# A hybrid GLA / S5 trunk on one core: z with both parts of u in one 512-column matmul, heads written in S5 order, background rates moved

## The chip, the cores and the metric

The program runs on one core of a Trainium2 chip. The metric is the device time of one execution in microseconds (us); lower is better. Runs of the kernel before: 1853.9, 1856.19 and 1862.4 us, median 1856.19.

## What is computed

Two layers on 256 tokens of width 2048, each a mixer with adaLN modulation around it and a LayerNorm after it. Layer 0 is gated linear attention (GLA), layer 1 an S5 state-space mixer. The part that the change touches is the first mixer:

```
u = x * (1 + scale) + shift                      # adaLN, from ada_w and c
q, k, v, z, g = split(u @ w_in)                  # 1024, 1024, 4096, 4096, 16 columns
o = chunked gated linear attention(q, k, v, g)   # 4 heads, 1024 values each
o = o * rsqrt(mean(o^2 over a head) + eps) * norm_g
h = (o * silu(z)) @ w_out
x = layer_norm(alpha * x + (1 + gate) * h)
```

The S5 layer projects the new x to its own u and z, runs the recurrence, multiplies gelu(y) by sigmoid(y @ w_glu + b), then by silu(z), and projects out.

## The kernel before

Everything large is a product with a weight matrix in float32 that must keep float32's accuracy. So each operand is cut in two parts of a shorter format: hi is the value cast, lo is the rest. `split` (L142) does that for each weight block of 2 x 128 rows by 512 columns: ScalarE casts hi (L145), VectorE subtracts to lo (L146). `hilo` (L327) does the same for activations. A product is then hi x hi + hi x lo + lo x hi, three matmuls.

Three helpers issue them. `mv_step` (L159) keeps the activations stationary and streams 512 weight columns. `st_step` (L171) keeps a 128 x 128 weight block stationary and streams 256 tokens: per feature block f (4) and k (2) it issues three matmuls of 256 columns (L180 to L182), all into the first half of a bank. `st_wide` (L184) streams hi and lo of the activations side by side in one matmul of 512 columns (L192), so that a bank's two halves hold two partial sums; a second matmul of 256 columns (L193) adds weight lo x activation hi to the first half. Whoever reads the bank must add the halves. `st_wide` needs activations in `Pairs` (hi and lo of each k next to each other), `st_step` takes `Parts` (hi tiles and lo tiles).

The stages, in order: u0 is made and v, q, k are projected in four blocks of k (`vqk_steps`, the last block runs 36 steps); the gate and the decayed state products follow (`gla_gate`, qs, sts); then the z stage, 8 groups of 512 columns with 8 steps each (L837 to L853); then `out_proj(0, ...)` with 4 column groups of 16 steps; then the S5 layer, whose GLU stage (L1241 on) uses `st_wide`. Inside the z stage the heads' work is taken from the queue `hq`: `o_step` makes 128 output features of a head and their squares, `rms` and `inv` the root and its reciprocal, `scale` multiplies, and `head_fin` multiplies by silu(z).

The S5 layer wants tokens in another order, (s c) with s = 8 steps of a chunk first. Before, z was written in that order by the Silu (L849), the heads' outputs stayed in token order, and `head_fin` (L833) read them with steps. PSUM has a pool `mm` of 5 banks; a z group holds 4 of them. Small tiles come from `s8`, 12 slots of 8 KB.

Besides the main work a list `bg` holds background items: 26 preparation items for S5, then 12 parts of the adaLN weights with 9 items each (`ada_dve`, L275: a load of 512 KB and two multiply-adds of 512 columns on VectorE, L292, or a closing item), 134 in all up to the end of `out_proj(0, ...)`. `pump(rate)` adds the rate to a counter and runs an item whenever it reaches 1. V_RATE holds in the last projection block (36 steps), Z_RATE in z (64), OP_RATE in the output projection (64). `issue_after(last_lo[0])` keeps an item's multiply-adds behind the newest lo on VectorE. What is written first has the better place, but the framework's planner orders each engine's instructions by that place and by its own costs; the engines then run their queues in order. Loads of weights go through SP's queue into a ring of buffers.

Of the kernel before, what the change touches and what calls it, by code (L numbers as in the profile page):

```python
# [8 lines left out]
F32 = mybir.dt.float32  # L9
F32R = mybir.dt.float32r  # L10
AF = mybir.ActivationFunctionType
# [4 lines left out]
P = 128  # L16
# [17 lines left out]
def trunk(ctx, tc, x, c, ln_g, ln_b, ada_w, ada_b, gla_w_in, gla_gate_w2, gla_gate_b, gla_norm_g,  # L34
# [39 lines left out]
    def s8t(name, shape, dt=F32):  # L74
        return s8.tile([P] + shape, dt, tag="s8", name=name)
# [95 lines left out]
    def st_step(banks, u, w, kp, last, first=0):  # L171

        hi, lo = w
        for f in range(4):
            for kk in range(2):
                k = 2 * kp + kk
                wh = hi[:, kk, f * P:(f + 1) * P]
                wl = lo[:, kk, f * P:(f + 1) * P]
                o = banks[f][:, :T]
                PE.matmul(o, lhsT=wh, rhs=u.hi(k), start=(k == first), stop=False)  # L180
                PE.matmul(o, lhsT=wh, rhs=u.lo(k), start=False, stop=False)  # L181
                PE.matmul(o, lhsT=wl, rhs=u.hi(k), start=False, stop=(k == last))  # L182

    def st_wide(banks, u, w, kp, last):  # L184


        hi, lo = w
        for f in range(4):
            for kk in range(2):
                k = 2 * kp + kk  # L190
                fs = slice(f * P, (f + 1) * P)
                PE.matmul(banks[f], lhsT=hi[:, kk, fs], rhs=u.both(k), start=(k == 0), stop=False)  # L192
                PE.matmul(banks[f][:, :T], lhsT=lo[:, kk, fs], rhs=u.hi(k), start=False, stop=(k == last))  # L193
# [128 lines left out]
        for tt in range(2):  # L322
            dma(xr[tt][:, c0:c1], x[0, tt * P:(tt + 1) * P, c0:c1])

    u0 = Parts([s8t(f"u0h{i}", [8, T], F32R) for i in range(2)], [s8t(f"u0l{i}", [8, T], F32R) for i in range(2)])

    def hilo(hi, lo, src):  # L327
        S.copy(hi, src)
# [313 lines left out]
    for part in range(2):  # L642
        for j in range(4):
            bg.extend(ada_dve(1, part, j))
    V_RATE, Z_RATE, OP_RATE = 0.825, 0.944, 0.755
    KEEP = (4, 6)
    GATE_AT = 15
    SCAN_RATE = 1.728
# [140 lines left out]
    y0 = Parts([], [])  # L789


    zt_ = [s8t(f"z{h}", [8, T]) for h in range(4)]
    og, sq = [None] * 4, [None] * 4

    def head(h):
        def o_step(vt_):
            if vt_ == 0:
                og[h] = s8t(f"og{h}", [8, T])
                sq[h] = tp.tile([P, T], F32, tag="sq", name=f"sq{h}", bufs=2)
            f = h * 8 + vt_  # L800
            ps = psx(f"pso{f}")
            PE.matmul(ps[:, 0:256], lhsT=vtok[:, 0, f * P:(f + 1) * P], rhs=sts[:, h, 0:256], start=True, stop=False)
            PE.matmul(ps[:, 128:256], lhsT=vtok[:, 1, f * P:(f + 1) * P], rhs=sts[:, h, 256:384], start=False, stop=True)
            S.activation(og[h][:, vt_, :], ps[:, :T], AF.Identity, scale=gnT[:, f:f + 1])
            if vt_ == 0:
                S.activation(sq[h], ps[:, :T], AF.Square)
            else:
                s_ = tp.tile([P, T], F32, tag="sqt", name=f"sqt{f}", bufs=2)
                S.activation(s_, ps[:, :T], AF.Square)
                V.tensor_tensor(sq[h], sq[h], s_, op=ALU.add)  # L810

        sd = {}

        def rms():
            ps = psx(f"psrms{h}")
            PE.matmul(ps[:, :T], lhsT=ones, rhs=sq[h], start=True, stop=True)
            sd[0] = tp.tile([P, T], F32, tag="sd", name=f"sd{h}", bufs=1)
            S.activation(sd[0], ps[:, :T], AF.Sqrt, scale=1.0 / 1024.0, bias=rmseps)

        def inv():  # L820
            V.reciprocal(sd[0], sd[0])

        def scale(i):
            o = og[h][:, 4 * i:4 * i + 4]
            V.tensor_tensor(o, o, sd[0].unsqueeze(1).to_broadcast([P, 4, T]), op=ALU.mult)

        return [lambda i=i: o_step(i) for i in range(8)] + [rms, inv] + [lambda i=i: scale(i) for i in range(2)]

    def head_fin(h):
        def step(i):  # L830
            sl = slice(4 * i, 4 * i + 4)
            zv = zt_[h][:, sl].rearrange("p f (s c) -> p f s c", s=8)
            V.tensor_tensor(zv, og[h][:, sl].rearrange("p f (c s) -> p f s c", s=8), zv, op=ALU.mult)  # L833
        return [lambda i=i: step(i) for i in range(2)]

    hq = []
    for g in range(8):  # L837
        if g % 2 == 0:
            hq += head(g // 2)
        banks = [psm(f"z{g}{f}") for f in range(4)]  # L840
        for kp in range(8):
            for _ in range(-(-len(hq) // (8 * (2 - g % 2) - kp))):
                hq.pop(0)()
            w = split(wload(win, 2 * kp, 6144 + g * 512, f"z{g}{kp}"), f"z{g}{kp}")
            st_step(banks, u0, w, kp, 15)
            pump(Z_RATE)
        for f in range(4):
            i = (g * 4 + f) % 8
            S.activation(zt_[g // 2][:, i, :].rearrange("p (s c) -> p c s", s=8), banks[f][:, :T].rearrange("p (c s) -> p c s", s=8), AF.Silu)  # L849
        if g % 2 == 1:  # L850
            hq += head_fin(g // 2)
            if g == 1:
                hq += conv(y0, zt_[0], "y0")  # L853
# [516 lines left out]
```

## Time and profile before

| | us |
|---|---|
| median of 3 runs | 1856.19 |
| profiled execution, device time | 1857.15 |
| its span (first to last instruction) | 1855.4 |
| TensorE busy | 1804.1 (97%) |
| VectorE busy | 1425.7 (77%) |
| ScalarE busy | 900.1 (49%) |

The profiled execution is a run of its own, 1.75 us longer than its span. A matmul's duration in the trace is longer than its share of the engine, because matmuls are pipelined: two that follow each other overlap. How fast they go is read from start to start. A row's square brackets hold the idle time of the engine just before the instruction, and what ended it.

### The profile page before, as it was taken

How to read it: one execution, taken by the hardware profiler on the slowest of the kernel's cores; microseconds unless marked ns; L12 is line 12 of the kernel's file. 1: busy time of each engine (PE TensorE's matmuls, PEld its weight loads, DVE VectorE, ACT ScalarE, POOL GpSimd, SP SyncE). 2: the span in 40 equal slices, each digit the busy share in tenths (PEclk: the TensorE clock that was granted, in tenths of full speed). 3: DMA queues.
4: the chain of work that ended last, by engine and by line, in shares of the span. 5: the costliest groups of instructions: out<-in, count | busy, mean ns of one | idle time of the engine just before them, and what ended most of it. 6: DMA issues, size and time to landing. Idle time of an engine off the chain costs nothing.

```text
span 1855.4 us, 33824 instructions
## 1 busy us (share of the span) xinstructions
PE 1804.1 (97%) x13619; PEld 1590.0 (86%) x13619; DVE 1425.7 (77%) x1890; ACT 900.1 (49%) x1252; POOL 65.0 (4%) x76
## 2 busy tenths in 40 slices
PE   6999999999999999999999999999999999999998
PEld 3787798799999888799998899998888888888886
DVE  2788675989989988688899779888677775557556
ACT  3533365655556333654444444555544444444332
POOL 0000000000000000002222110000000000000000
PEclk9999999999999999999999999999999999999998
DMA  9887976689889998565555477899788886668653
GB/s 357 316 270 249 348 252 210 216 296 325 284 287 316 334 352 285 174 199 165 157 164 157 123 207 217 238 241 248 226 271 263 277 272 211 191 187 328 194 188 91
DMA packets 239525, 449.21 MB, mean 242 GB/s; under 512 B 19236, under 2 KB 45278, under 8 KB 238086
## 3 DMA queue, kind: packets, MB, share of 16 engines
q1 hardware_dynamic: 235432, 437.59, 73.5%
q0 software_dynamic: 3168, 8.41, 1.4%
q8 instruction: 107, 1.75, 0.4%
q10 hardware_dynamic: 768, 1.05, 0.2%
q14 instruction: 50, 0.41, 0.1%
HBM read 432.55 MB, written 14.42 MB: 241 GB/s over the span
## 4 chain that ended last, share of the span: by engine, by line
PE 75%; DVE 5%; DMA 3%; ACT 1%; issue 1%; SPq 0%; DVEq 0%; ACTq 0%
PE gl L192 13%; PE gl L193 7%; PE op L168 6%; PE op L169 6%; PE op L167 6%; PE z L182 3%; PE z L180 3%; PE z L181 3%; PE sz L180 3%; PE sz L182 3%; PE sz L181 3%; PE su L180 2%; PE su L181 2%; PE su L182 2%; DMA rb<-rec 1%; PE pswb L1018 1%
## 5 line engine op out<-in xcount | busy, mean ns | idle before, releaser
L146 DVE TENSOR_TENSOR logl<-wgl,higl 128x1024 fp32r<-128x1024 f32 x128 | 156.5, 1224 | 114.7 <-ACT higl L145 113.3
L145 ACT CAST higl<-wgl 128x1024 fp32r<-128x1024 f32 x128 | 134.8, 1054 | 171.2 <-PE gl L192 160.3
L192 PE MATMUL gl<-yp,higl 128*128 128x512 f32 x512 | 179.1, 395 | 0.1
L192 PE MATMUL gl<-yb,higl 128*128 128x512 f32 x512 | 179.1, 395 | 0.0
L145 ACT CAST hio<-wo 128x1024 fp32r<-128x1024 f32 x96 | 101.4, 1057 | 155.1 <-PE op L169 137.2
L146 DVE TENSOR_TENSOR loo<-wo,hio 128x1024 fp32r<-128x1024 f32 x96 | 117.3, 1223 | 65.3 <-ACT hio L145 63.3
L292 DVE SCALAR_TENSOR_TENSOR acc<-wa,cs,acc 128x512 f32<-128x512 f32 x215 | 160.9, 748 | 2.8
L180 PE MATMUL su<-u1h,hisu 128*128 128x256 f32 x512 | 153.0, 300 | 0.0
L180 PE MATMUL sz<-u1h,hisz 128*128 128x256 f32 x512 | 149.6, 292 | 1.2 <-ACT zs L1201 1.2
L180 PE MATMUL z<-u0h,hiz 128*128 128x256 f32 x512 | 148.7, 290 | 0.0
L181 PE MATMUL su<-u1l,hisu 128*128 128x256 f32 x512 | 147.1, 287 | 0.0
L182 PE MATMUL su<-u1h,losu 128*128 128x256 f32 x512 | 146.6, 286 | 0.0
L182 PE MATMUL z<-u0h,loz 128*128 128x256 f32 x512 | 145.0, 283 | 0.9 <-DVE loz L146 0.9
L182 PE MATMUL sz<-u1h,losz 128*128 128x256 f32 x512 | 144.8, 283 | 0.3 <-DVE losz L146 0.3
L181 PE MATMUL sz<-u1l,hisz 128*128 128x256 f32 x512 | 144.8, 283 | 0.0
L181 PE MATMUL z<-u0l,hiz 128*128 128x256 f32 x512 | 144.7, 283 | 0.0
L193 PE MATMUL gl<-yb,logl 128*128 128x256 f32 x512 | 143.1, 280 | 0.0
L193 PE MATMUL gl<-yp,logl 128*128 128x256 f32 x512 | 141.8, 279 | 0.0
L145 ACT CAST hisz<-wsz 128x1024 fp32r<-128x1024 f32 x64 | 67.0, 1052 | 100.1 <-PE sz L181 61.7
L192 PEld LDWEIGHTS gl<-yb,higl 128*128 128x128 f32 x512 | 96.0, 187 | 22.4
L192 PEld LDWEIGHTS gl<-yp,higl 128*128 128x128 f32 x512 | 95.8, 188 | 22.6 <-issue 0.6
L145 ACT CAST hisu<-wsu 128x1024 fp32r<-128x1024 f32 x64 | 66.9, 1050 | 94.3 <-PE su L181 80.1
(321 smaller groups left out, 5025.6 us busy)
## 6 DMA issues: line engine op xcount, KB each, us to landing
wgl<-in_s_w_glu SPq DMA_DIRECT2D x128, 512.0 KB, 4.9
wa<-in_ada_w SPq DMA_DIRECT2D x115, 512.0 KB, 5.2
a<-in_ada_w SPq DMA_DIRECT2D x32, 1024.0 KB, 11.6
wv<-in_gla_w_in SPq DMA_DIRECT2D x64, 512.0 KB, 5.3
wz<-in_gla_w_in SPq DMA_DIRECT2D x64, 512.0 KB, 5.0
wsu<-in_s_w_in SPq DMA_DIRECT2D x64, 512.0 KB, 3.8
wsz<-in_s_w_in SPq DMA_DIRECT2D x64, 512.0 KB, 4.6
wo<-in_s_w_out SPq DMA_DIRECT2D x64, 512.0 KB, 4.8
```

Of the source, the lines that this page charges most:

```text
L145: S.copy(hi, w)
L146: last_lo[0] = V.tensor_tensor(lo, w, hi.bitcast(F32), op=ALU.subtract).ins
L167: PE.matmul(banks[tt], lhsT=uh, rhs=hi[:, kk, :], start=(k == first), stop=False)
L168: PE.matmul(banks[tt], lhsT=uh, rhs=lo[:, kk, :], start=False, stop=False)
L169: PE.matmul(banks[tt], lhsT=ul, rhs=hi[:, kk, :], start=False, stop=(k == last))
L180: PE.matmul(o, lhsT=wh, rhs=u.hi(k), start=(k == first), stop=False)
L181: PE.matmul(o, lhsT=wh, rhs=u.lo(k), start=False, stop=False)
L182: PE.matmul(o, lhsT=wl, rhs=u.hi(k), start=False, stop=(k == last))
L192: PE.matmul(banks[f], lhsT=hi[:, kk, fs], rhs=u.both(k), start=(k == 0), stop=False)
L193: PE.matmul(banks[f][:, :T], lhsT=lo[:, kk, fs], rhs=u.hi(k), start=False, stop=(k == last))
L292: V.scalar_tensor_tensor(acc[0], w[:, kk, :], cs[:, k:k + 1], acc[0], op0=ALU.mult, op1=ALU.add)
L1018: PE.transpose(ps[:, g * P:(g + 1) * P], wu[p][:, f % 2, 4 * h + g].rearrange("p i s -> p (i s)"), ident)
```

## The change

In the z stage `st_step` becomes `st_wide`, and u0 becomes `Pairs`. A bank's second half is copied to a buffer by ScalarE, VectorE adds the first half, and the Silu reads the sum. The heads' outputs and the root are written in S5 order by ScalarE, so that `head_fin` multiplies without steps. The three rates of the background list are changed.

```diff
-    u0 = Parts([s8t(f"u0h{i}", [8, T], F32R) for i in range(2)], [s8t(f"u0l{i}", [8, T], F32R) for i in range(2)])
+    u0 = Pairs([s8t(f"u0p{i}", [4, 2, T], F32R) for i in range(4)])
...
-    V_RATE, Z_RATE, OP_RATE = 0.825, 0.944, 0.755
+    V_RATE, Z_RATE, OP_RATE = 0.9, 0.78, 0.82
...
+    def steps_first(ap):
+        return ap.rearrange("p (s c) -> p c s", s=8)
+
+    def by_chunk(ap):
+        return ap.rearrange("p (c s) -> p c s", s=8)
...
-            S.activation(og[h][:, vt_, :], ps[:, :T], AF.Identity, scale=gnT[:, f:f + 1])
+            S.activation(steps_first(og[h][:, vt_, :]), by_chunk(ps[:, :T]), AF.Identity, scale=gnT[:, f:f + 1])
...
-            S.activation(sd[0], ps[:, :T], AF.Sqrt, scale=1.0 / 1024.0, bias=rmseps)
+            S.activation(steps_first(sd[0]), by_chunk(ps[:, :T]), AF.Sqrt, scale=1.0 / 1024.0, bias=rmseps)
...
-            zv = zt_[h][:, sl].rearrange("p f (s c) -> p f s c", s=8)
-            V.tensor_tensor(zv, og[h][:, sl].rearrange("p f (c s) -> p f s c", s=8), zv, op=ALU.mult)
+            V.tensor_tensor(zt_[h][:, sl], og[h][:, sl], zt_[h][:, sl], op=ALU.mult)
...
-            st_step(banks, u0, w, kp, 15)
+            st_wide(banks, u0, w, kp, 15)
...
-            S.activation(zt_[g // 2][:, i, :].rearrange("p (s c) -> p c s", s=8), banks[f][:, :T].rearrange("p (c s) -> p c s", s=8), AF.Silu)
+            zl = tp.tile([P, T], F32, tag="uf", name=f"zl{g}{f}", bufs=2)
+            S.copy(zl, banks[f][:, T:])
+            V.tensor_tensor(zl, banks[f][:, :T], zl, op=ALU.add)
+            S.activation(steps_first(zt_[g // 2][:, i, :]), by_chunk(zl), AF.Silu)
```

## Rows read from the trace of the kernel before

**Rows 1.** The page's first part: busy us, share of the span, instructions.

```profile
PE 1804.1 (97%) x13619; PEld 1590.0 (86%) x13619; DVE 1425.7 (77%) x1890; ACT 900.1 (49%) x1252; POOL 65.0 (4%) x76
```

**Rows 2.** Windows by stage: stretch, length, busy us by engine (count), clock, DMA.

```profile
core 0: us, PE busy (x) PEld busy (x) DVE busy (x) ACT busy (x) POOL busy (x), PEclk, DMA share, GB/s
260.00:369.50 109.50, 107.89 (x597) 90.91 (x599) 84.40 (x105) 69.67 (x74) 5.80 (x5) 0.98 0.73 232
369.50:589.00 219.50, 218.57 (x1768) 213.29 (x1769) 196.28 (x237) 129.90 (x201) 0.00 (x0) 1.00 0.89 304
589.00:769.00 180.00, 179.89 (x813) 148.57 (x812) 152.23 (x188) 73.69 (x76) 0.00 (x0) 1.00 0.86 293
1307.70:1667.60 359.90, 359.82 (x2057) 314.03 (x2057) 237.96 (x280) 173.11 (x218) 0.00 (x0) 1.00 0.75 240
```

**Rows 3.** Groups in 369.5 to 589: shapes, count, busy us, mean ns, idle before.

```profile
L146 DVE TENSOR_TENSOR loz<-wz,hiz 128x1024 fp32r<-128x1024 f32 x64 | 78.1, 1221 | 19.9 <-ACT hiz L145 19.9
L292 DVE SCALAR_TENSOR_TENSOR acc<-wa,cs,acc 128x512 f32<-128x512 f32 x101 | 75.5, 748 | 1.3
...
L849 ACT ACTIVATE z<-z 128x256 f32<-128x256 f32 x31 | 17.8, 680 | 0.2
L804 ACT ACTIVATE og<-pso,vt 128x256 f32<-128x256 f32 x32 | 15.0, 468 | 0.6 <-PE pso L803 0.6
L833 DVE TENSOR_TENSOR z<-og,z 128x1024 f32<-128x1024 f32 x7 | 15.0, 2139 | 0.2 <-ACT z L849 0.2
...
L825 DVE TENSOR_TENSOR og<-og,sd 128x1024 f32<-128x1024 f32 x8 | 9.5, 1218 | 0.0
```

**Rows 4.** PE's timeline in z (start, us): two starts, 87 matmuls apart.

```profile
430.07 0.28 PE L182 MATMUL z<-u0h,loz 128*128 128x256 f32 x1
...
440.51 0.28 PE L182 MATMUL z<-u0h,loz 128*128 128x256 f32 x1
```

**Rows 5.** PE's timeline in z: the largest late start.

```profile
414.01 0.39 PE L182 MATMUL z<-u0h,loz 128*128 128x256 f32 x1 [0.65 <-DVE loz L146]
```

**Rows 6.** PE's timeline in the GLU stage: 21 pairs apart, a group's end, 15 apart.

```profile
1344.65 0.39 PE L192 MATMUL gl<-yb,higl 128*128 128x512 f32 x1
...
1351.93 0.39 PE L192 MATMUL gl<-yb,higl 128*128 128x512 f32 x1
...
1399.78 0.28 PE L193 MATMUL gl<-yp,logl 128*128 128x256 f32 x1
1400.14 0.47 PE L192 MATMUL gl<-yp,higl 128*128 128x512 f32 x1
...
1400.56 0.40 PE L192 MATMUL gl<-yp,higl 128*128 128x512 f32 x1
...
1405.86 0.40 PE L192 MATMUL gl<-yp,higl 128*128 128x512 f32 x1
```

**Rows 7.** Tile gl: duration ns least/median/greatest, first and last start.

```profile
L1259 ACT ACTIVATE sg<-gl,vt x32: 453/468/479, 1350.5 to 1672.0; 128x256 f32<-128x256 f32 x32
L1260 DVE TENSOR_TENSOR sg<-gl,sg x32: 403/418/426, 1351.8 to 1673.3; 128x256 f32<-128x256 f32 x32
```

**Rows 8.** End of the projections: a window, VectorE's last qs, PE's chain of waits.

```profile
333.00:369.50 36.50, 36.50 (x175) 29.66 (x175) 36.50 (x47) 22.09 (x23) 2.31 (x2) 1.00 0.72 228
...
367.78 1.24 DVE L759 TENSOR_TENSOR qs<-qk,ft 128x1024 f32<-128x1024 f32 x1
...
369.46 5.34 PE psst L773 x52
```

**Rows 9.** A window in the projections.

```profile
320.00:330.00 10.00, 8.39 (x31) 6.05 (x30) 9.99 (x12) 9.00 (x11) 0.00 (x0) 0.85 0.26 80
```

**Rows 10.** Output projection: a window, and ScalarE's timeline.

```profile
620.00:680.00 60.00, 59.89 (x268) 49.26 (x268) 51.01 (x63) 22.68 (x22) 0.00 (x0) 1.00 1.04 385
...
623.78 1.06 ACT L145 CAST hio<-wo 128x1024 fp32r<-128x1024 f32 x1 [3.29 <-DMA wo<-in_gla_w_out]
```

**Rows 11.** VectorE's timeline at the end of the output projection.

```profile
763.38 0.69 DVE L867 TENSOR_TENSOR ot<-op,gate 128x512 f32<-128x512 f32 x1 [3.12 <-PE op L169]
```

## The prediction

> **What bounds the kernel now.** I first read the page's table of engines: TensorE is busy for 97% of the span [rows 1], but that alone doesn't say where a microsecond can be gained. So the windows by stage come next [rows 2]: the end of the projections (260 to 369.5 us), the z stage that the change rewrites (369.5 to 589), the GLA output projection (589 to 769), and the S5 GLU stage (1307.7 to 1667.6), which already runs the 512-column form. In the z stage PE is busy for 218.6 of 219.5 us at full granted clock (1.00, the 2.4 GHz level), VectorE for 196.3, ScalarE for 129.9. PE sets the length, and VectorE is close behind. The groups of instructions of that stretch [rows 3] give the prices of what is added and removed there. Last, PE's timeline, read by start to start because durations of pipelined matmuls overlap: in z, 87 matmuls of 256 columns start within 440.51 - 430.07 = 10.44 us, so 0.120 us each [rows 4]; one feature block and one k need three of them, 0.360 us. Late starts are few; the largest is a matmul 0.65 us late for its loz [rows 5].
>
> **The change part by part.** *The matmuls.* Per pair (f, k) three matmuls of 256 columns become one of 512 and one of 256; the columns stay 768. In the GLU stage that pair repeats after (1351.93 - 1344.65) / 21 = 0.347 us in one stretch and (1405.86 - 1400.56) / 15 = 0.353 us in another [rows 6]. The whole stage with everything else in it is 359.9 us for 1024 pairs, 0.3515 [rows 2]. I take 0.3495, between the fast stretch and the stage. There are 8 groups x 8 steps x 4 f x 2 = 512 pairs: 512 x (0.3600 - 0.3495) = 5.4 us less; the ends are 512 x 0.007 = 3.4 and 512 x 0.013 = 6.8 us less.
>
> *A rule weighed.* The two stretches show that the 512-column matmul costs 0.347 - 0.120 = 0.227 us, less than two of 256 [rows 4, 6]. The Trainium skill, "TensorE: Matmul & The Clock Gate", section "Back-to-back issue gap", gives a warm gap of N / 2.4 + 2.5 ns. By it three matmuls of 256 would take 328 ns and the new pair 325, an estimate of 1.3 us saved in all instead of 5.4. The trace disagrees with the first of these: 360 ns, not 328.
>
> *Reading the bank.* For each of the 32 banks one ScalarE copy of 256 columns and one VectorE add are new; the Silu stays. The GLU stage has the same pair at 0.468 and 0.418 us [rows 7]: ScalarE +15.0, VectorE +13.4 us. Against that, on VectorE, the final product of a head becomes unstepped: the stepped one takes 2.139 us, the plain product of the same 1024 elements 1.218 [rows 3]. Seven lie in this stage: -6.4 us. Z_RATE from 0.944 to 0.78 takes 64 x 0.164 = 10.5 background items out of it, each two multiply-adds of 0.748 us [rows 3]: -15.7 us. VectorE's sum goes from 196.3 to 196.3 + 13.4 - 6.4 - 15.7 = 187.6 us in about 214, the same share as before. The stepped writes move to the heads' outputs on ScalarE: 32 x (0.680 - 0.468), the stepped Silu against the plain output [rows 3] = +6.8 us, the roots about +1. ScalarE ends near 153 of 214. Neither becomes the bound; PE's work hides all of it. If that cover failed, a group's end would pay it (rival 2).
>
> At the seven inner group ends the next group needs the banks. Five banks exist, four are in use, so new block f needs old block f-1. In the GLU stage, with the same chain (copy, add, function) and two buffers as here, one late start is seen, 0.36 - 0.12 = 0.24 us [rows 6]. I take 0.1 us for each of the seven: +0.7 us, ends 0 and 1.7. The late starts of before [rows 5] I leave as they are: reciprocal, scaling and lo stay in one VectorE queue.
>
> *Head outputs and root in S5 order.* The squares are still summed in token order, and the ones-matmul is unchanged; only what is written moves. Nothing on PE.
>
> *u0 in pairs.* Four tiles of 8 KB instead of four: no slot and no instruction is added. 0.
>
> *V_RATE 0.825 to 0.9.* In the last projection block of 36 steps 32 items are popped instead of 29 (floor of 32.4 and 29.7): the 26 preparation items some two steps sooner, and three more ada items, 3 x 2 x 0.748 = 4.5 us of VectorE, each with a 512 KB load in SP's queue between those of wv. They fall into a stretch where VectorE is busy for 36.5 of 36.5 us [rows 8]. Behind it waits the scaled q for the state: its last product ends at 367.78 + 1.24 = 369.02, and PE starts the state at 369.46 [rows 8]. So 0.44 us of slack, then PE waits, unless the planner puts the multiply-adds behind q or z's first step ahead of the state. Upper end 4.5 - 0.4 = +4.1. Below, a gain is possible too: at 320 to 330 PE loses 1.6 us and runs at a mean clock of 0.85 [rows 9]; earlier preparation could loosen that. Lower end -1.6 - 1.5 (the missing 0.15 of 10 us) = -3.1. I take +1.0, nearer the middle, since z's loads are free to fill.
>
> *OP_RATE 0.755 to 0.82.* The list has 26 + 12 x 9 = 134 items. Before, 36 x 0.825 + 64 x 0.944 = 90.1 are due by the end of z, so 44 are left; now 32.4 + 49.9 = 82.3, so 52 are left. Eight more items in the output projection: 8 x 1.5 = 12 us of VectorE, which has 180 - 152.2 = 28 us idle [rows 2], and 4.2 MB of loads. From 620 to 680 the DMA engines are full (share 1.04, 385 GB/s), and ScalarE already waited 3.29 us for a load of wo at 623.78 [rows 10]. The higher rate adds 16 x 0.065 = 1.04 items, 0.54 MB, in the first 16 steps, 1.4 us at 385 GB/s. PE had used up its lead there, so 0 to +1.4; I take +0.5. The list now ends with pump 64 (51.7 / 0.82 = 63.0) instead of pump 59 ((134 - 90.1) / 0.755 = 58.1), so the last ada part lies among the late steps, ahead of the LayerNorm. VectorE was idle there for 3.12 us before the gated product [rows 11]: 0 to +1.5, taken as +0.3. Together +0.8.
>
> Sum: -5.4 + 0.7 + 1.0 + 0.8 = -2.9 us. The profiled execution takes 1857.15 us (span 1855.4 and 1.75 around it), so 1854.25; it lies 0.96 above the median of the runs (1856.19), so the forecast is 1853.3 us. The stages after 769 us have their own waits and get no term.
>
> **Rivals.** (1) *Only columns count.* The columns are 768 before and after; if the stream alone is priced, the matmuls give 0 and the sum is +2.5 us: 1858.7. For it: the slow GLU stretch is only 2% below z [rows 4, 6]. Against it: all GLU spacings lie below 0.360. By the skill's gap formula named above it would be +1.2 us, 1857.4.
>
> (2) *Slower: the banks come free too late.* Place: each inner group end. Copy 0, copy 1, add 0, Silu 0, copy 2 (two buffers, so it waits for Silu 0), add 2. If each add stands behind one lo (1.221) and one multiply-add (0.748) [rows 3], that is 0.47 + 1.97 + 0.42 + 0.68 + 0.47 + 1.97 + 0.42 = 6.4 us. It starts when block 0 is complete, three blocks of 0.7 us before the group's end, and must be over three blocks after it: 4.2 us. So up to 2.2 us late; at 1.5 us each, 10.5 in all, in place of the 0.7: 1853.3 - 0.7 + 10.5 = 1863.1. It decides from (2.9 + 0.7) / 7 = 0.5 us per end. For it: VectorE is busy for 89% here and for 66% in the GLU stage [rows 2]. Against it: the same chain cost the GLU stage 0.24 us once [rows 6], and the planner may put blocks of later steps first.
>
> (3) *The jam at 320 to 330 goes.* Preparation two steps earlier meets the gate's functions at another moment; with -3.1 instead of +1.0 the time is 1849.2. For it: PE's only clearly broken stretch in the projections lies there [rows 9]. Against it: the gate starts at the same step as before, and the load that the products wait for moves along with them.
>
> **How the numbers follow.** Chances: forecast 0.58, rival 1 0.14, rival 2 0.13, rival 3 0.15. About 0.5% (9.3 us) is what a measurement of this kernel tells from no change: faster means below 1846.9, slower above 1865.5. The forecast's own ends are -6.8 us with nothing given back (1849.4) and -3.4 + 1.7 + 4.1 + 1.4 + 1.5 = +5.3 us (1861.5); that all four costs come in full is unlikely, so its own range is 1849 to 1860. Rival 3 with the 6.8 us end and nothing given back is 1856.2 - 6.8 - 3.1 = 1846.3; that, and stretches that I leave as they are, make 0.13. Rival 2 at 2.2 us per end gives 15.4 us and 1868; that and a planner that turns out worse elsewhere: 0.07. Within: 0.80. The range for 8 in 10 leaves out the tails of rivals 2 and 3: 1845 to 1861.
>
> **What would show it.** The matmuls: starts of the 512-column z matmuls 0.347 to 0.353 us apart, the z stage some 5 us shorter; 0.36 would be rival 1. The banks: waits of PE for the new add at the seven group ends; over 0.5 us each is rival 2. The rates: PE's first state matmul waiting for qs, and the stretch 320 to 330 again, for V; ScalarE's waits for wo near 620 and the idle time ahead of the last gated product for OP. VectorE busy for about 188 us in z. Wrong would be a z stage not shorter than 217 us, or a change of more than 5 us after 769 us, where nothing is edited.

## The result, and the profile after

The changed kernel takes 1861.22 us (median of 12 runs) against 1857.2 for the kernel before on the same chip (12 runs): ratio 1.0025, 95% interval 1.0015 to 1.0035, so by the ratio about 4.6 us slower (the medians differ by 4.0). The forecast was 2.9 us faster, with a range up to 1861. Its profiled execution took 1859.1 us, span 1857.3.

The windows by stage, answering to [rows 2] (stretch, length, busy us by engine with counts, clock, DMA share and GB/s):

```profile
260.00:369.50 109.50, 103.03 (x583) 86.80 (x582) 84.16 (x105) 70.70 (x77) 6.71 (x6) 1.00 0.72 231
369.50:589.00 219.50, 216.95 (x1261) 186.65 (x1260) 193.28 (x252) 144.17 (x227) 0.00 (x0) 1.00 0.84 283
589.00:769.00 180.00, 179.89 (x817) 148.82 (x816) 156.55 (x198) 73.60 (x77) 0.00 (x0) 1.00 0.92 312
```

The z stage's matmuls go as forecast: PE's timeline has two starts of a 512-column matmul 17 pairs apart, (445.59 - 439.69) / 17 = 0.347 us per pair instead of 0.360 [rows 4].

```profile
439.69 0.40 PE L192 MATMUL z<-u0p,hiz 128*128 128x512 f32 x1
...
445.59 0.39 PE L192 MATMUL z<-u0p,hiz 128*128 128x512 f32 x1
```

The loss lies around it: ahead of z, where PE is busy for 4.9 us less in the window 260 to 369.5 than before, and behind z, where the output projection and the LayerNorm take longer. The state's first matmul starts at 374.03 instead of 369.46 [rows 8], and z's first while VectorE still has the last qs to do (PE, then VectorE):

```profile
374.03 2.80 PE L773 MATMUL psst<-qs,qk 128*64 128x256 f32 x24
376.77 0.73 PE L192 MATMUL z<-u0p,hiz 128*128 128x512 f32 x2
```

```profile
375.75 1.22 DVE L759 TENSOR_TENSOR qs<-qk,ft 128x1024 f32<-128x1024 f32 x1
```

To place gains and losses I cut every trace at the first start of a few matmuls, in us: **block** is the last projection block, from its first transpose of x to the first state matmul; **z** from there to the first matmul of the output projection; **op** from its first to its last matmul; **tail** from there to the first matmul of the S5 layer (su); **S5** from su to the first of the GLU stage. Each length is from one profiled execution; the median and the ratio are from all runs.

| run | median | ratio to before [95%] | block | z | op | tail | S5 |
|---|---|---|---|---|---|---|---|
| before | 1857.2 | | 127.7 | 219.7 | 179.3 | 6.0 | 533.4 |
| after | 1861.22 | 1.0025 [1.0015, 1.0035] | 131.3 | 216.4 | 180.4 | 7.9 | 531.9 |
| e1 after, old rates | 1856.45 | 0.9997 [0.9983, 1.0011] | 127.6 | 219.1 | 179.2 | 6.2 | 535.6 |
| e2 before, new rates | 1866.59 | 1.0050 [1.0032, 1.0069] | 131.0 | 220.5 | 180.7 | 7.9 | 532.1 |
| e3 wide only | 1861.01 | 1.0023 [1.0008, 1.0038] | 127.7 | 220.4 | 180.6 | 6.0 | 531.8 |
| e4 S5 order only | 1857.06 | 0.9999 [0.9984, 1.0014] | 126.4 | 219.8 | 179.1 | 6.2 | 536.4 |
| e5 V_RATE only | 1863.05 | 1.0034 [1.0020, 1.0048] | 132.3 | 219.6 | 178.7 | 6.1 | 539.1 |
| e6 as e5, six items without loads | one run | | 130.7 | 219.8 | 178.7 | 6.0 | 542.4 |
| e7 as e5, six items loads only | one run | | 131.0 | 221.4 | 178.8 | 6.2 | 541.5 |
| e8 rates between | 1862.61 | 1.0030 [1.0016, 1.0043] | 127.7 | 216.3 | 179.7 | 7.7 | 538.2 |
| e9 before, pacer 0.136 | 1861.15 | 1.0013 [0.9998, 1.0027] | 126.4 | 219.7 | 179.3 | 6.2 | 544.4 |
| e10 as e8, pacer 0.436 | 1859.41 | 1.0004 [0.9987, 1.0020] | 127.7 | 216.4 | 180.6 | 7.7 | 535.9 |
| e11 best, Z_RATE 0.86 | 1856.35 | 0.9986 [0.9974, 0.9999] | 127.7 | 214.1 | 183.5 | 6.2 | 528.1 |
| e12 the same, 0.9 | 1857.9 | 0.9998 [0.9986, 1.0009] | 127.7 | 216.2 | 182.0 | 6.2 | 535.8 |
| e13 preparation sooner | one run | | 130.7 | 219.6 | 181.0 | 6.2 | 534.7 |
| e14 as e11, x by columns | 1857.6 | 1.0002 [0.9986, 1.0018] | 127.7 | 214.2 | 182.4 | 7.5 | 531.5 |
| e15 as e11, V_RATE 0.76 | 1858.69 | 1.0012 [0.9999, 1.0026] | 127.8 | 218.3 | 183.1 | 6.2 | 529.6 |
| e16 as e11, preparation early | 1861.74 | 1.0024 [1.0009, 1.0038] | 131.9 | 214.9 | 183.1 | 6.2 | 533.6 |
| e17 as e11, eight items loads only | 1857.85 | 1.0009 [0.9996, 1.0022] | 127.7 | 214.3 | 183.4 | 6.2 | 533.4 |
| e18 as e11, eight items without loads | 1854.84 | 0.9991 [0.9973, 1.0009] | 127.6 | 213.8 | 181.6 | 6.0 | 539.7 |

One of e11's 12 executions took 4054.2 us and is not in its ratio.

Equal code gives equal stages to a few tenths of a microsecond (block 127.6 or 127.7 in the nine with Pairs and V_RATE 0.825), the S5 column excepted. The changed kernel against before: block +3.6, z -3.3, op +1.0, tail +1.9, and 1.0 that came ahead of the block, where nothing was edited: su starts at 778.7 instead of 774.4, 4.3 us later. Behind su its profile is 2.4 us shorter, most of it in the S5 column, which varies as much between equal code.

Not all of z's -3.3 comes from the wide form. The closing item of an ada part runs eight small matmuls (psmod) on PE, and the new rates moved one such item from z to op. These are psmod's groups in z, before and after; in op there are 40 before and 48 after. Eight of them take 0.8 us from start to next start, so 0.8 of z's gain, and 0.8 of op's +1.0, are this one item:

```profile
L236 PE MATMUL psmod<-ones,acc 128*128 128x1 f32 x24 | 2.9, 240 | 0.0
L236 PE MATMUL psmod<-ones,acc 128*128 128x1 f32 x16 | 1.9, 240 | 0.0
```

### The profile page after: what moved, and what is told of

The parts are those of the page before. It is cut to its first block, busy times and chain, and to the rows that moved or that the text cites. A ratio compares the mean times of both kernels' runs of the same rounds, so it can differ in the third digit from the quotient of the medians.

```text
span 1857.3 us, 32877 instructions
## 1 busy us (share of the span) xinstructions
PE 1800.2 (97%) x13107; PEld 1561.7 (84%) x13107; DVE 1428.5 (77%) x1922; ACT 912.6 (49%) x1284; POOL 68.0 (4%) x76
## 4 chain that ended last, share of the span: by engine, by line
PE 80%; DVE 7%; DMA 6%; ACT 4%; issue 2%; SPq 0%; DVEq 0%; ACTq 0%
PE gl L192 13%; PE gl L193 6%; PE op L168 5%; PE op L169 5%; PE op L167 5%; PE z L192 5%; PE sz L180 3%; PE sz L182 3%; PE sz L181 3%; PE z L193 3%; PE su L180 2%; PE v L168 2%; PE su L181 2%; PE su L182 2%; PE v L169 2%
## 5 line engine op out<-in xcount | busy, mean ns | idle before, releaser
L192 PE MATMUL z<-u0p,hiz 128*128 128x512 f32 x512 | 184.3, 403 | 1.4 <-ACT hiz L145 1.4
L192 PE MATMUL gl<-yb,higl 128*128 128x512 f32 x512 | 178.7, 394 | 0.0
L292 DVE SCALAR_TENSOR_TENSOR acc<-wa,cs,acc 128x512 f32<-128x512 f32 x209 | 156.3, 748 | 4.2 <-DMA wa<-in_ada_w 1.9
L193 PE MATMUL z<-u0p,loz 128*128 128x256 f32 x512 | 142.3, 280 | 0.8 <-DVE loz L146 0.8
L192 PEld LDWEIGHTS z<-u0p,hiz 128*128 128x128 f32 x512 | 96.0, 188 | 22.8 <-ACT hiz L145 1.7
```

Source lines behind the costliest of these rows:

```text
L292: V.scalar_tensor_tensor(acc[0], w[:, kk, :], cs[:, k:k + 1], acc[0], op0=ALU.mult, op1=ALU.add)
```

## The experiments

**Which part costs: e1 to e4.** e1 is the changed kernel with the rates of before, e2 the kernel before with the new rates, e3 the wide form alone (Pairs, `st_wide`, halves added), e4 the S5 order alone.

```diff
-    V_RATE, Z_RATE, OP_RATE = 0.9, 0.78, 0.82
+    V_RATE, Z_RATE, OP_RATE = 0.825, 0.944, 0.755   # e1; e2 is the reverse in the kernel before
```

> The changed kernel with the three rates of before (0.825, 0.944, 0.755). Theory R (the rates cost what was lost: more background loads share ring, queue and VectorE with the last projection block, and the list ends too late in the output projection): first state matmul back at 369 to 370 us, z stage some 3 to 5 us shorter than before, LayerNorm after the output projection as before; time 3 to 6 us below the kernel before, ratio 0.997 to 0.998. Theory E (reading the bank's halves costs it): the ratio stays at 1.002 or above. VectorE is fuller in z here (10 items more), so late starts at group ends could take 1 to 3 us of it back.

> The kernel before with the three new rates (0.9, 0.78, 0.82), nothing else. Theory R: first state matmul at about 374 us, output projection some 1 us longer and its LayerNorm some 2 us longer; 5 to 9 us slower than before, ratio 1.003 to 1.005. Theory E: no difference beyond 0.1%.

> The kernel before with u0 in pairs, the 512-column matmul and the halves added, old rates, heads still in token order. Theory R: z stage 3 to 5 us shorter, time 2 to 5 us below before, ratio 0.997 to 0.999. Theory E: slower than before by 2 to 5 us.

> The kernel before with heads' outputs and root written in S5 order, old rates and old matmuls. Both theories: z stage within 1 us of before, since PE bounds it; VectorE's product 1.2 instead of 2.1 us, ScalarE's output 0.7 to 0.75 instead of 0.47 us; ratio 0.999 to 1.0005.

The rates are the loss: without them the change is no slower than before (e1), and they alone cost the kernel before 0.5% (e2). The wide form alone is slower (e3): with the stepped product of 2.139 us [rows 3] and 32 adds of 0.42 us in z on VectorE, z and op are each over 1 us longer than in e1. The S5 order alone gives nothing (e4). So most likely it is what makes the adds bearable, and only in the pair. With the old rates the pair gives nothing either: z's matmuls take 189.3 us in e1, from each start to the next start on PE, as many as before, and VectorE is busy for 200.6 of the 219.1 us of z.

**V_RATE: e5, e6, e7, e13.** e5 is e1 with V_RATE 0.9. In e6 the first six ada items read a tile that is there instead of loading; in e7 they load, but multiply and add 8 columns. So neither computes the gate's values. e13 pops at 0.9 but stops at 29 items in that block, as many as before; its other rates and the pacer's fraction (below) are those of before.

```diff
+                early6 = (l, part, j) == (0, 2, 0) and kp < 6     # e6: no load; e7: 8 columns
...
-                pump(V_RATE)
+                if len(bg) > 134 - 29:                            # e13
+                    pump(V_RATE)
```

> The changed kernel with V_RATE left at 0.9 and the other two rates of before (0.944, 0.755): the list ends near pump 55 of the output projection, earlier than before. Theory (V_RATE is the greater loss, and the tail of the output projection comes from the list's late end): from the gate's first matmul (psglr) to the first state matmul 71 to 72 us, as in the changed kernel (71.2) and not as with the old rates (68.0); from the last op matmul to su 6.0 to 6.2 us, not 7.9; time some 1859 to 1860, 2 to 3 us over before. Rival (the loss came from Z_RATE and OP_RATE, V_RATE is only seen in the order): 68 to 69.5 us there, time 1856 to 1857.

> As the run with V_RATE 0.9 alone, but the first six items of the first ada part (three of which V_RATE puts into the last projection block, three into the state's stretch) read a tile that is already there instead of loading 512 KB each; the multiply-adds stay, the values of that gate part are wrong. Theory A (the loads, in SP's queue and in the ring of six buffers, make wv late): gate to first state matmul 68 to 69.5 us. Theory B (the 4.5 us of VectorE's multiply-adds delay the products and low parts that PE needs): 71 to 72 us as with the loads.

> As the run with V_RATE 0.9 alone, but the same six items do their loads and multiply-adds of 8 columns in place of 512, so VectorE's time for them goes (0.748 us each to about 0.1) and the buffers come free at once; the values of that gate part are wrong. Theory A (loads): 71 us or more from the gate to the first state matmul. Theory B (VectorE's time): 68 to 69.5 us. If both this run and the one without loads lie below 69.5, it takes both: a load whose buffer is freed late.

> The changed kernel with V_RATE 0.9 but only 29 items popped in the last projection block, as before: the 26 preparation items come two steps sooner, the three more ada items do not come there; other rates of before, pacer at 0.436 after the list. Theory A (the three more items pay): from the gate's first matmul to the first state matmul 68 to 69 us. Theory B (the preparation's earlier place pays): 70.5 to 72. From the runs without the items' loads (70.5) and without their VectorE time (70.9), each with a stretch of granted clock 0.83 in it that costs some 1.7 us by itself, I expect 68.5 to 69.5: mostly A, with 1 us for the jam that moved from 324 to 336 us.

e5 shows that V_RATE makes the block longer, 127.6 to 132.3. But e6 and e7 take off only 1.6 and 1.3 (all three with one 10 us stretch at a mean clock of 0.83), and e13, with no item more than before, still has 130.7. So the three more items, which I had priced, are the smaller part: the changed kernel, which has them, takes 131.3 in that block and e13 130.7, both at a granted clock of 1.00. My own mixed expectation for e13 was wrong too, and its theory B holds: the earlier place of the 26 preparation items (and of the three ada items behind them) is what costs. ScalarE's timeline of the changed kernel shows how:

```profile
321.85 1.03 ACT L145 CAST hiv<-wv 128x1024 fp32r<-128x1024 f32 x1
...
323.15 1.05 ACT L585 COPY rowsb<-psrb 128x512 f32<-128x512 f32 x1
...
324.48 1.28 ACT L689 ACT_TABLE_LOAD   x1
...
326.83 0.99 ACT L585 COPY rowsb<-psrb 128x512 f32<-128x512 f32 x1
...
327.99 1.04 ACT L629 COPY cc<-cin 128x1024 f32<-128x1024 f32 x1
329.05 1.28 ACT L686 ACT_TABLE_LOAD   x1
...
331.31 1.03 ACT L145 CAST hiv<-wv 128x1024 fp32r<-128x1024 f32 x1
332.25 1.06 ACT L630 ACTIVATE cc<-cin 128x1024 f32<-128x1024 f32 x1
333.32 1.28 ACT L689 ACT_TABLE_LOAD   x1
...
335.67 1.05 ACT L585 COPY rowsb<-psrb 128x512 f32<-128x512 f32 x1
336.52 2.00 ACT L145 CAST hiv<-wv 128x1024 fp32r<-128x1024 f32 x2
```

The preparation's copies (rowsb, cc, 1 us each) now stand among the gate's functions and their table loads, and between 321.85 and 336.52 only one hi cast of v gets through, where PE uses one every 2.7 us (12 matmuls, six of which start within 336.05 - 334.68 = 1.37 us). In e1 the gate's last function of this kind stands ahead of the copies of rowsb and cc, and four hi casts of v follow between 332 and 340 us:

```profile
329.66 1.15 ACT L689 ACTIVATE ea<-ea,ones 128x1024 f32<-128x1024 f32 x1
330.72 1.06 ACT L585 COPY rowsb<-psrb 128x512 f32<-128x512 f32 x1
```

In e13 ScalarE goes through the same order as in the changed kernel. In the changed kernel PE then waits for the cast, and 20 us later for a lo that stands behind the first qs (2.30 us) and two sums of v on VectorE (PE, then VectorE):

```profile
337.63 0.49 PE L167 MATMUL v<-hiv,u0p 128*128 128x512 f32 x1 [1.19 <-ACT hiv L145]
...
359.80 0.50 PE L168 MATMUL v<-lov,u0p 128*128 128x512 f32 x1 [1.84 <-DVE lov L146]
```

```profile
354.46 2.30 DVE L759 TENSOR_TENSOR qs<-qk,ft 128x2048 f32<-128x2048 f32 x1
356.66 1.29 DVE L364 TENSOR_TENSOR vbig<-vbig,v 128x512 f32<-128x512 f32 x2
357.86 0.76 DVE L292 SCALAR_TENSOR_TENSOR acc<-wa,cs,acc 128x512 f32<-128x512 f32 x1
358.52 1.23 DVE L146 TENSOR_TENSOR lov<-wv,hiv 128x1024 fp32r<-128x1024 f32 x1
```

e1 has a jam of its own at 320 to 330 us, 8.42 us busy, where e13 has 9.57. In the next two windows shown, e1 is at 10.00 and 10.00 and e13 at 7.51 and 8.42; over 320 to 370 PE is busy for 48.3 us in e1 and 45.3 in e13, about the 3.1 us of the block (e1, then e13):

```profile
320.00:330.00 10.00, 8.42 (x37) 5.93 (x36) 9.05 (x12) 8.97 (x11) 0.00 (x0) 1.00 0.32 104
330.00:340.00 10.00, 10.00 (x51) 8.43 (x50) 10.00 (x13) 9.17 (x10) 0.00 (x0) 1.00 0.56 164
350.00:360.00 10.00, 10.00 (x52) 8.25 (x51) 10.00 (x12) 6.27 (x8) 0.00 (x0) 1.00 0.66 211
```

```profile
330.00:340.00 10.00, 7.51 (x36) 5.79 (x35) 8.07 (x11) 9.96 (x11) 0.00 (x0) 1.00 0.34 105
350.00:360.00 10.00, 8.42 (x39) 6.60 (x38) 10.00 (x16) 6.17 (x8) 1.15 (x1) 1.00 0.64 190
```

**Is another place better: e15, e16.** Both start from e11 (below). e15 pops more slowly, e16 at 1.7 and no more than 29 items, so that the preparation is done when the gate begins.

```diff
-    V_RATE, Z_RATE, OP_RATE = 0.825, 0.86, 0.9
+    V_RATE, Z_RATE, OP_RATE = 0.76, 0.86, 0.95      # e15
+    V_RATE, Z_RATE, OP_RATE = 1.7, 0.86, 0.9        # e16, with e13's stop
```

> The version with Z_RATE 0.86, the Sqrt behind the Silus and the pacer at 0.436, with V_RATE 0.76 in place of 0.825 (27 items in the last projection block; OP_RATE 0.95 keeps the list's end near pump 54). Theory (the four copies of the preparation must not stand between the gate's functions on ScalarE): they now come two to three steps later still, behind the gate's functions, so the late starts near 324 us (0.84 and 1.05 us) shrink or go: from the gate's first matmul to the first state matmul 66 to 67.5 us in place of 68.0, time 1 us less, 1855. Rival: the preparation now meets the running sums and the products of q and k on VectorE, and the state waits: 69 to 71 us, time 1858.

> The same version with V_RATE 1.7, stopped at 29 items: the preparation is done by step 16 of the 36, when the gate has just begun, and ScalarE's copies of it come ahead of the gate's functions. Theory as above: the gate's stretch has room, the late starts near 324 us go, gate to first state matmul 66 to 67.5 us; but the preparation at twice the pace costs ScalarE and VectorE before the gate: from the block's first matmul to the gate's 60 to 62 in place of 59.7. Sum -1 to +1, time 1855.5 to 1857.5. Rival (a denser preparation jams the casts as the gate did): 63 or more there, time 1859 or more.

No: 127.8 and 131.9. PE's loss only moves: in e15 it is gone from 320 to 330 us, and PE is busy for 9.17 and 9.35 us in the two windows of 10 us behind; in e16 it is 7.93 us at 280 to 290 and 8.34 at 340 to 350. The pace of before is as good as any tried.

**The tail, and the rates of z and op: e8, e10.** e8 keeps V_RATE at 0.825 and lets the list end late. e10 is e8 with the pacer's fraction as before (below).

```diff
+    V_RATE, Z_RATE, OP_RATE = 0.825, 0.86, 0.785    # e8, e10
```

> The changed kernel with V_RATE 0.825 of before and rates 0.86 and 0.785, so that the list still ends at pump 63 or so of the 64 in the output projection, as in the changed kernel, while the last projection block has the list of before. Theory: gate to first state matmul 68 us (as with the old rates), last op matmul to su 7.9 us and the first to the last op matmul 180.4 against 179.2, so that the time is 3 us over the run with the old rates, some 1859.5. Rival (the tail comes of the wide matmul or of V_RATE's order): last op matmul to su 6.0 to 6.3 us, time 1856.5.

> The run with the rates 0.825, 0.86, 0.785 (1862.6 us, though it reached su at 774.0 against 774.4 before), with the pacer set to 0.436 after the list, the fraction that the kernel before has there (it had 0.98). Theory: the stages after su as before, 533 us from su to gl in place of 538; time 1857 to 1858.5. Rival (something else in the wide form costs it 5 us behind 774 us): 1862.

Block 127.7, tail 7.7: the two losses come apart as expected, V_RATE makes the first, the list's end at pump 63 the second (in e11 and e12, which end near 55 and 58, the tail is 6.2; only e14, which loads parts of x late, has a list that ends near 55 and a tail of 7.5). The changed kernel's timelines show the path: a cast waits for a late load of wo, and the first gated product comes at 768.97, 1.8 us ahead of the start of PE's last op matmul, where before it came at 763.38 [rows 11], 5.0 us ahead; in e12 it comes at 762.27, again 5.0 us ahead (ScalarE and VectorE of the changed kernel, then VectorE of e12):

```profile
760.15 1.05 ACT L155 CAST hio<-wo 128x1024 fp32r<-128x1024 f32 x1 [4.41 <-DMA wo<-in_gla_w_out]
```

```profile
768.97 0.69 DVE L876 TENSOR_TENSOR ot<-op,gate 128x512 f32<-128x512 f32 x1 [0.52 <-PE op L169]
```

```profile
762.27 0.69 DVE L878 TENSOR_TENSOR ot<-op,gate 128x512 f32<-128x512 f32 x1 [3.13 <-PE op L169]
```

The five traces with a tail over 7 us (after, e2, e8, e10, e14) share one more thing. The LayerNorm's root needs a table on ScalarE. Where the tail is near 6, its load starts 8.9 to 9.4 us ahead of PE's last op matmul, and the first half's root 2.5 us ahead. In the five, ScalarE first does one or two more casts for the next stage, the last of which waits for PE; the load starts from 1.2 us ahead to 1.5 us behind, and the first root 0.1 to 2.8 us behind. In e14 the first half's mean was computed 2.2 us ahead of PE's last op matmul, and its root still came behind it. Which share the order on ScalarE has, and which the late first half, is not shown (before, then after):

```profile
759.02 1.28 ACT L884 ACT_TABLE_LOAD   x1
772.30 1.28 ACT L893 ACT_TABLE_LOAD   x1
```

**The pacer's fraction: e9.** e8 reached su at 774.0, sooner than before, and was still 0.3% slower. The counter that pops the list keeps its fraction, and the S5 stages pop their scans by the same counter: 36 x 0.825 + 64 x 0.944 + 64 x 0.755 = 138.436 before, 134.80 after, 141.136 in e5, 134.98 in e8. The planned order behind the LayerNorm follows it: on ScalarE it is one and the same in before, e1, e3 and e4, and another in e5 to e7. e9 is the kernel before with one line:

```diff
     while bg:
         pump()
+    pace[0] = 0.136
```

> The kernel before, with one number set: when the background list is empty after the output projection, the pacer that pops the list's items (a running sum of the rates, of which the whole part is popped) is set to 0.136. Its fraction at that point is what the three rates leave over: 36 x 0.825 + 64 x 0.944 + 64 x 0.755 = 138.436 before, 134.80 after, 141.136 with V_RATE alone. Nothing ahead of the LayerNorm is touched. Theory (the fraction sets at which steps of the S5 stages the scans are issued, and so the planned order there; 0.136 is a bad one, which is why the run with V_RATE alone lost 2 us more than the changed kernel): the stages from su to the GLU some 4 to 8 us longer than with 0.436 (533.3 us from su to gl before), time 1860 to 1863. Rival (those stages vary from run to run and the kernel has no part in it): 1856 to 1858, as before.

Its planned order there is that of e5, and PE waits for the loads of mt in it:

```profile
1238.21 0.42 PE L1175 MATMUL psy<-mt,U 128*32 128x128 f32 x8 [2.80 <-DMA mt<-dk]
...
1282.83 0.42 PE L1175 MATMUL psy<-mt,U 128*32 128x128 f32 x8 [3.95 <-DMA mt<-dk]
```

Such waits for mt sum to 7.5 us in e9 and 3.4 to 6.6 in e5 to e7, against 0 to 3.9 in the traces at 0.436, so they are a part of it at most. The four traces at 0.136 (e5, e6, e7, e9) have S5 at 539.1 to 544.4, mean 541.9; the thirteen at 0.436 have 528.1 to 539.7, mean 533.8. The time says +2.4 us with an interval from -0.4 to +5.0, and e10 against e8 points the same way (ratio 1.0004 against 1.0030). So the fraction 0.136 most likely costs some microseconds; the runs don't settle how many. The changed kernel's own 0.80 shows no such cost (531.9).

**A version meant to be faster: e11, e12.** V_RATE of before, fewer items in z, the list ended in time, the pacer's fraction of before, and one more edit: the root's Sqrt is issued behind the group's last Silu.

```diff
+    V_RATE, Z_RATE, OP_RATE = 0.825, 0.86, 0.9      # e12: 0.825, 0.9, 0.8
...
+            with tc.issue_after(last_silu[0]):
+                S.activation(steps_first(sd[0]), by_chunk(ps[:, :T]), AF.Sqrt, scale=1.0 / 1024.0, bias=rmseps)
...
+            last_silu[0] = S.activation(steps_first(zt_[g // 2][:, i, :]), by_chunk(zl), AF.Silu).ins
```

> A version meant to be faster than both: the changed kernel with V_RATE 0.825 (last projection block as before), Z_RATE 0.86 (VectorE gets room for the adds), OP_RATE 0.9 (the list ends near pump 55 of the output projection), the pacer set to 0.436 after it, and the root's Sqrt issued behind the group's last Silu. By the stages of the runs so far: 369.3 to the first state matmul, 216.3 less 1 to 2 for the Sqrt, 179.2 to 180.5 in the output projection, 6.1 behind it, then as before: some 3.5 to 4.5 us less than before, 1853. What could spoil it: the higher rate in the output projection meets full DMA engines at 620 to 680 us (+1 to +2), or the Sqrt behind the Silus is late for the final product; then 1855.

> The same with Z_RATE 0.9 and OP_RATE 0.8: the list ends near pump 58 as before, the output projection carries two items more than before, and z two items fewer. If the z stage needs VectorE's room only at the group ends, 216 us as well, and the output projection 179.3, so 1853; if the late starts in z grow with the rate in proportion (219.1 us at 0.944, 216.3 at 0.86), 217.5 less 1 to 2, so 1854.

The Sqrt was behind the two large late starts in the changed z stage. ScalarE loads three tables in a row at the first group's end, and the next hi casts stand behind them; PE loses 1.36 us, then 0.84 for the lo (ScalarE, then PE):

```profile
407.90 1.28 ACT L858 ACT_TABLE_LOAD   x1
...
410.86 1.28 ACT L825 ACT_TABLE_LOAD   x1
412.16 0.73 ACT L825 ACTIVATE sd<-psrms,kst 128x256 f32<-128x256 f32 x1
412.90 1.28 ACT L858 ACT_TABLE_LOAD   x1
...
415.12 2.00 ACT L145 CAST hiz<-wz 128x1024 fp32r<-128x1024 f32 x2
```

```profile
416.23 1.19 PE L192 MATMUL z<-u0p,hiz 128*128 128x512 f32 x4 [1.36 <-ACT hiz L145]
418.26 0.39 PE L193 MATMUL z<-u0p,loz 128*128 128x256 f32 x1 [0.84 <-DVE loz L146]
```

In e11 two loads are left, with a cast between them, and PE's wait is 0.32:

```profile
401.68 1.28 ACT L860 ACT_TABLE_LOAD   x1
...
404.50 1.06 ACT L145 CAST hiz<-wz 128x1024 fp32r<-128x1024 f32 x1
...
406.67 1.28 ACT L827 ACT_TABLE_LOAD   x1
```

```profile
415.68 0.39 PE L193 MATMUL z<-u0p,loz 128*128 128x256 f32 x1 [0.32 <-DVE loz L146]
```

The Trainium skill, "ScalarE: Activation LUTs", section "Rules for kernel authors", says to do all functions of one table set before switching; here the trace agrees. The same page of the Trainium skill, section "What ACT_TABLE_LOAD costs", counts 1283 ns and a drain of some 1380 ns per switch; the load is 1.28 us here, but the next function starts 414.20 - 412.90 = 1.30 us after the load's start, so no such drain stands behind it.

z falls to 214.1, 5.6 us under before (0.8 of it the closing item), yet e11 gains only 0.14% (interval 0.01% to 0.26%), some 2.6 us, and e12 nothing: op takes 183.5 and 182.0. From the first state matmul to su e11 is only 1.2 us shorter than before, and e17, equal to e11 in these stages to 0.3 us, measured a ratio of 1.0009; so even this gain is not certain.

**Where z's gain goes: e14, e17, e18.** z, op and tail together are 405.0 before and 404.7 after, and 403.8 to 405.2 in all versions with V_RATE 0.825 but e3 (407.0), however z and op share it, until loads are taken away (e18, 401.5). In e11's op ScalarE waits 5.91 us for a load of wo:

```profile
621.55 1.06 ACT L145 CAST hio<-big 128x1024 fp32r<-128x1024 f32 x1 [5.91 <-DMA big<-in_gla_w_out]
```

e14 loads x in four column groups, so that 1.5 MB leave that stretch. e17 and e18 halve the background items there: eight of them load but compute 8 columns (e17), or compute without loading (e18); so neither computes all modulation values.

```diff
-        hooks[0, 12 + t] = [lambda t=t: [dma(res0[t][32 * s:32 * s + 32], xv[4 * t + s]) for s in range(4)]]
+        for cg in range(4):                              # e14
+            sl = slice(cg * 512, (cg + 1) * 512)
+            hooks[cg, 12 + t] = [lambda t=t, sl=sl: [dma(res0[t][32 * s:32 * s + 32, sl], xv[4 * t + s][:, sl]) for s in range(4)]]
...
+            light = kp in {(1, 0, 3): (6, 7), (1, 1, 0): (1, 4, 7), (1, 1, 1): (1, 4, 7)}.get((l, part, j), ())   # e17, e18
```

> The version with 0.825, 0.86, 0.9, the Sqrt behind the Silus and the pacer at 0.436 (z stage 214.1 us, output projection 183.5, 1856.35 us), in which x (2 MB, read at steps 12 and 13 of the output projection) is loaded in four column groups, each with the quarter of the output that needs it: 1.5 MB leave the stretch 620 to 680 us, where the DMA engines are full at 386 GB/s, 3.9 us of their time. Theory (that stretch holds the output projection's end): the late starts there (0.98, 0.49, 0.80 us, and ScalarE's 5.9 us wait for a load of wo) mostly go, the output projection takes 181 to 182 us, the time falls by 1.5 to 2.5 us to 1854 to 1855. Rival (VectorE, at 0.9 of a background item per step, holds it, through lo): 183.5 and 1856.4 again.

> The version with 0.825, 0.86, 0.9, the Sqrt behind the Silus and the pacer at 0.436, in which eight ada items of the output projection's first half load as before but multiply and add 8 columns in place of 512 (eight times 1.5 us of VectorE go; the values of those modulation columns are wrong). If VectorE's queue (lo behind the multiply-adds) is what holds the output projection: 180 to 181 us in place of 183.5, the first state matmul to su 401 to 402 in place of 403.8, time some 2 to 3 us under that version's 1856.35. If the loads hold it: 183 to 183.5 and 1856.

> The same version with the same eight items without their loads of 512 KB (they read a small tile that is there), all of VectorE's work kept; the values are wrong. If the full DMA engines at 620 to 680 us hold the output projection: 180 to 181 us in place of 183.5, ScalarE's 5.9 us wait for wo near 621 us gone; 4.2 MB less are 10.9 us of DMA time at 386 GB/s. If VectorE holds it: 183 us. Spreading the loads of x took 1.1 us off (182.4) and the waits for DMA near 620, so I expect about half here, 181.5 to 182.5, and half in the run without the multiply-adds.

The windows 620 to 680 us of e11, e17 and e18, in this order:

```profile
620.00:680.00 60.00, 58.21 (x262) 47.29 (x262) 51.71 (x66) 23.20 (x22) 0.00 (x0) 1.00 1.05 386
```

```profile
620.00:680.00 60.00, 58.26 (x263) 47.51 (x262) 44.89 (x65) 23.16 (x22) 0.00 (x0) 1.00 1.05 386
```

```profile
620.00:680.00 60.00, 59.18 (x269) 48.72 (x268) 54.51 (x69) 22.15 (x21) 0.00 (x0) 1.00 0.95 345
```

e17 frees VectorE (44.89 instead of 51.71) and nothing moves: op 183.4. e18 frees the DMA engines (345 instead of 386 GB/s), PE's busy time rises by 1 us there, and op falls to 181.6. So in e11 it is the loads, not VectorE, and I had expected half of each. e14 took the long wait away but only 1.1 us off op, and its tail grew to 7.5; its time is that of before. Loads are not all of it: e18 is still 2.4 us over the 179.2 of e1. An item's closing matmuls are 0.8 us of that: 48 psmod matmuls stand among op's in e11 and in the changed kernel, 40 in before and e1.

## Why the prediction was wrong

The step that failed is the V_RATE term; the late end of the list was priced too low as well. The terms in turn:

**The matmuls, -5.4: right.** 0.347 us per pair, inside the ends. From each z matmul's start to the next start on PE, z's matmuls sum to 189.3 us before and 186.4 after; without the late starts over 0.13 us (2.4 and 4.1) that is 186.9 and 182.3, so -4.6. Rival 1 (only columns count) is out. The z stage of 216.4 us lies just under the 217 that I had named as a sign of being wrong, and only with the moved closing item's 0.8 in it. VectorE was busy for 190.0 us of it, near the 187.6 of the forecast.

**Reading the banks, +0.7: measured +1.7, at another place.** The adds cost no start over 0.4 us at the seven group ends; rival 2 is out. The late starts rose because the planner put the Sqrt between the Silus of the first group; I had priced the root as 1 us of ScalarE and left its table out. And Z_RATE is needed: at 0.944 the late starts are 5.9, with the same two behind the Sqrt (1.37 and 0.83), and z is 219.1 (e1).

**u0 in pairs, 0: wrong by about 1.2.** Block is 126.4 with Parts (e4, e9) and 127.6 to 127.8 with Pairs at 0.825; PE's idle time ahead of the preparation's transposes pspw shows it (e4, then e1):

```profile
L570 PE MATMUL pspw<-ident,pd 128*128 128x128 f32 x32 | 4.2, 274 | 0.7 <-ACT lc L572 0.7
```

```profile
L570 PE MATMUL pspw<-ident,pd 128*128 128x128 f32 x32 | 4.3, 278 | 2.0 <-ACT lc L572 1.1 <-ACT pd L563 0.9
```

Why the casts come later there is not shown. In the profile of before this is hidden by the 0.85 of clock at 320 to 330 [rows 9], which e4 does not have with the same code there. So the block's +3.6 is 1.2 for the pairs and 3.7 for V_RATE, less 1.3 that before lost to its clock: that it comes close to V_RATE's own cost is luck.

**V_RATE, +1.0: the step that failed.** It measured +3.7 (131.3 against e1's 127.6), within the upper end that I gave and did not take. I priced the three more items, 4.5 us of VectorE behind the scaled q, and moved "the 26 preparation items some two steps sooner" without asking what they meet. I weighed that only as a gain (the lower end -3.1, rival 3). It was the cost: the copies meet the gate's functions on ScalarE (e13). The jam didn't go, it moved from 324 to 336 us and a second one at 358 came behind it.

**OP_RATE, +0.8: measured +2.9**, +1.0 in op and +1.9 in the tail. Of the +1.0 the moved closing item is 0.8, which I had not priced; op's own matmuls took 175.5 us instead of 175.3, so the backlog of loads, my +0.5, shows as 0.2 here. It is real in e11. The late end of the list I took as +0.3 of a possible 1.5. It took away the cover under which the first half was normalized, and with it ScalarE's early table load.

**The sum.** I added the terms as if z's gain and op's cost were separate. They are linked: the list's items leave z for op. In the changed kernel 0.8 of z's -3.3 came back in op as a closing item, and the late list cost 1.9 in the tail; in e11, with more items in op's first half, the loads took it (e18). With z -3.3 against op and tail +2.9, what is left is the block's +3.6, where I had put +1.0.

**Behind 769 us no term.** Right for this pair, not in general: the rates reach the S5 stages through the pacer's fraction (e9).

## What to carry to other kernels

A rate of background work is a choice of place, not only of amount: list for each moved item what it will stand next to on every engine, also the items that are merely sooner. Where a list is fixed, a microsecond won in one stage by sending work to the next is won only if the next has room on the resource that the work uses; in e11 that was the loads (e17, e18). And measure rates apart from the rewrite that they come with: the rewrite here changed the time by -0.03% with the old rates (interval -0.17% to +0.11%), and by -0.14% with rates and a table switch fitted to it (e11, interval -0.26% to -0.01%).

## What the runs showed of the hardware

The granted clock falls in some runs of the same code and not in others. In the stretch of PE's late starts at 320 to 330 us it was busy for 8.39 us at a clock of 0.85 in the kernel before [rows 9], a mean over its two levels of 2.4 and 1.2 GHz; in e4, with the same code up to there, for 8.38 us at 1.00:

```profile
320.00:330.00 10.00, 8.38 (x37) 6.27 (x37) 10.00 (x12) 8.99 (x11) 0.00 (x0) 1.00 0.25 74
```

e9, whose code is that of before up to the LayerNorm, has 8.43 at 1.00. Block is 127.7 in before and 126.4 in e4 and e9, so such a stretch is worth 1.3 us here, as much as several of the terms that were argued over. In the same way PE was busy for 7.53 us of 330 to 340 in the changed kernel and for 7.52 in e6, and the clock of the ten us behind it was 1.00 and 0.83.
